# A hybrid decoder layer on one core: merge gates moved into a phase of their own, made by Strassen's seven block products

## The chip, the cores and the metric

The kernel runs on one core of a Trainium2 chip. The core has TensorE (PE) for matmuls, VectorE (DVE), ScalarE (ACT), GpSimd (POOL) and SyncE (SP), which here issues every DMA. The metric is the time of one execution in microseconds on the device, the median of three runs.

## What is computed

One step of a decoder layer for 1056 tokens: 1024 of a prompt and 8 x 4 of a decode batch, with shared weights. Cut to what matters here:

```python
xn = rmsnorm(x, norm_mix)
proj = xn @ w_in            # 1024 -> 512 (B) | 512 (C) | 512 (h) | 1536 (q,k,v) | 512 (z) | 8 | 512 (q_mem) | 3 x 1024 gates
y_a  = b_gate * causal_conv(c_gate * h_in)                    # branch A
o_dn = rmsnorm(gated_delta_chunked(q, k, v, g, beta, s0))     # branch B: a recurrence over chunks
y_dn = o_dn * jax.nn.silu(z)
y_m  = mem_attention(xq, mk, mv)                              # branch M
merged = (jax.nn.sigmoid(g_a) * (y_a @ w_branch[:512])
          + jax.nn.sigmoid(g_dn) * (y_dn @ w_branch[512:1024])
          + jax.nn.sigmoid(g_m) * (y_m @ w_branch[1024:]))
x = x + merged @ w_o
gate, up = jnp.split(rmsnorm(x, norm_ffn) @ w_up, 2, axis=-1)
y = rmsnorm(x + (jax.nn.silu(gate) * up) @ w_down, norm_final)
```

New convolution and recurrence states and the memory's keys and values are returned too.

## The kernel before

All large products are exact to float32 by three matmuls in fp32r: a weight and an activation are each split into a high and a low part (`split`: ScalarE casts the high part, VectorE subtracts), and high x high, high x low and low x high are added in one PSUM bank. `X` holds both parts of the normed input, transposed (8 tiles of 128 channels by 1056 tokens). `proj` (lines 266 to 277) makes 128 output columns over one of three token tiles `TT` (384, 384 and 288 tokens): 8 channel tiles by three matmuls, 24 in all, at lines 274 to 276.

The program has four stages. *The weave* (up to line 1119) lays four streams of work into each other by a clock of guessed costs (`weave`, `UNIT`, and the factors `SCS`, `DNS`, `ATS`); a scheduler then orders each engine's instructions by priority against a simulated timeline. The streams are: `bulk_all`, plain column products in the sequence of the string `ORDER` (X: the memory branch's queries, K: memory keys and values, L: a DeltaNet head's q, k, v, A: branch A, M and B: gates and branch products of the memory branch and branch A, G: gates of the DeltaNet branch, Z: its z columns); `dn_prep_all`, for each of 8 halves (4 heads by 2) a triangular inverse, whose 31 steps on VectorE (`dn_solve`, lines 489 to 491) run between two trips through DRAM, then `dn_levels` on TensorE; `dn_scan_all`, the recurrence; and `att_all`, attention and the decode tokens. In this stage matmuls of the three latter streams stand between the bulk's, on TensorE's in-order queue.

In the weave, `branch` (1009 to 1032) makes for each of 8 column tiles the gate (24 matmuls a token tile, then sigmoid, line 1024) and the branch product (12 a token tile), multiplies them and stores the result in DRAM (`dM`, `dAo`). `gate_d` (1034) keeps 8 gate tiles of the DeltaNet branch in SBUF (`sgD`), and `z_part` (984) makes y = o * silu(z).

*The merge* (1163 to 1183) makes the DeltaNet branch's products, multiplies them with `sgD`, adds `dM` and `dAo`, and splits the sum into `X`. Then *w_o with the second norm* (from 1296), *up* (from 1352) and *down* (from 1522). The up projection already takes seven block products for eight: `up_pieces` makes the sums of weight blocks, `combine` those of activations (T1 to T4), and `up_chunk` has the products, each 4 channel tiles by three matmuls on 256 or 272 tokens (lines 1425 to 1427). For it the late stages have four raw weight buffers and eight piece buffers (`ring_t`).

## Time and profile before

| | us |
|---|---|
| median of 3 runs (1891.04 to 1895.27) | 1892.73 |
| the profiled execution | 1891.13 |
| its span | 1889.4 |
| PE busy | 1851.5 |
| DVE busy | 1060.4 |
| ACT busy | 707.1 |
| POOL busy | 133.0 |

The span runs from the first to the last instruction of the profiled execution. A matmul's busy time is from its issue to the modelled end of its results, and overlaps the next; the distance between starts is what it costs in a stream. The weave lasts to 998 us, where the merge's first matmul stands; w_o begins at 1045 us, up at 1146 us and down at 1611 us.

### The profile page before, as it was taken

What the parts mean: (1) busy time and instruction counts of PE and PEld (TensorE: products, weight loads), DVE (VectorE), ACT (ScalarE), POOL (GpSimd) and SP (SyncE); (2) the same over time, 40 slices, a digit from 0 to 9 for tenths busy, and PEclk for the clock granted to TensorE, in tenths of its full rate; (3) what the DMA queues carried; (4) which work ended last, traced back from release to release, by engine and by line L of the source; (5) the groups of instructions that cost most, each with busy time, mean ns of one, the idle gap of its engine ahead of it and who ended that gap; (6) DMA issues with size and microseconds to landing.
All of it is one profiled execution on the core that took longest, in us unless ns stands there. A gap on an engine that the chain in (4) does not pass through costs nothing.

```text
span 1889.4 us, 31322 instructions
## 1 busy us (share of the span) xinstructions
PE 1851.5 (98%) x12193; PEld 1719.1 (91%) x12193; DVE 1060.4 (56%) x2543; ACT 707.1 (37%) x1520; POOL 133.0 (7%) x234
## 2 busy tenths in 40 slices
PE   6999999999999999999999999999999999999997
PEld 6799999889999999999999879999999999787776
DVE  6666568454744357721137567666766668536224
ACT  5533453234423343233232366433333335433121
POOL 3100011010100012100005000000000000001000
PEclk9999999999999999999999999999999999999999
DMA  5123122341322215431155445232323234846321
GB/s 175 34 71 82 48 62 78 114 138 52 110 74 80 89 42 136 125 94 55 52 171 170 162 149 186 73 94 72 94 72 94 74 93 149 271 142 211 107 85 65
DMA packets 224705, 200.43 MB, mean 106 GB/s; under 512 B 21332, under 2 KB 182025, under 8 KB 224556
## 3 DMA queue, kind: packets, MB, share of 16 engines
q1 hardware_dynamic: 224556, 198.43, 34.0%
q8 instruction: 95, 1.56, 0.4%
q14 instruction: 54, 0.44, 0.1%
HBM read 160.27 MB, written 38.12 MB: 105 GB/s over the span
## 4 chain that ended last, share of the span: by engine, by line
PE 93%; DVE 2%; DMA 2%; ACT 1%; issue 1%; SPq 0%; DVEq 0%; ACTq 0%
PE psb L274 14%; PE psb L275 13%; PE psb L276 13%; PE psb L1427 7%; PE psb L1425 7%; PE psb L1426 7%; PE psb L1281 6%; PE psb L1280 6%; PE psb L1282 6%; PE psb L1364 2%; DMA x<-in_x_prompt_dram 1%; PE psa L926 1%; PE psb L1284 1%; PE psb L1285 1%; PE psa L906 1%
## 5 line engine op out<-in xcount | busy, mean ns | idle before, releaser
L274 PE MATMUL psb<-x,whi 128*128 128x384 f32 (+1 forms) x1272 | 418.3, 329 | 1.6 <-ACT whi L103 1.2
L276 PE MATMUL psb<-x,wlo 128*128 128x384 f32 (+1 forms) x1272 | 415.1, 328 | 0.5 <-DVE wlo L96 0.5
L275 PE MATMUL psb<-x,whi 128*128 128x384 f32 (+1 forms) x1272 | 415.3, 327 | 0.0
L96 DVE TENSOR_TENSOR pc<-raw,pc 128x512 fp32r<-128x512 f32 (+1 forms) x237 | 198.0, 845 | 155.8 <-ACT pc L103 153.8
L103 ACT CAST pc<-raw 128x512 fp32r<-128x512 f32 (+1 forms) x237 | 174.0, 745 | 260.6 <-PE psb L1281 115.2
L274 PEld LDWEIGHTS psb<-x,whi 128*128 128x128 f32 x1272 | 239.6, 188 | 5.3 <-issue 1.9
L276 PEld LDWEIGHTS psb<-x,wlo 128*128 128x128 f32 x1272 | 239.9, 189 | 3.3 <-DVE wlo L96 1.2
L275 PEld LDWEIGHTS psb<-x,whi 128*128 128x128 f32 x1272 | 239.8, 189 | 3.1 <-issue 2.0
L96 DVE TENSOR_TENSOR wlo<-raw,whi 128x1024 fp32r<-128x1024 f32 x73 | 90.6, 1241 | 111.1 <-ACT whi L103 107.0
L1426 PE MATMUL psb<-bx,pc 128*128 128x272 f32 (+1 forms) x480 | 136.4, 285 | 0.0
L1427 PE MATMUL psb<-bx,pc 128*128 128x272 f32 (+1 forms) x480 | 136.3, 286 | 0.0
L1281 PE MATMUL psb<-pc,hx 128*128 128x512 f32 x344 | 136.1, 396 | 0.0
L1425 PE MATMUL psb<-bx,pc 128*128 128x272 f32 (+1 forms) x480 | 135.9, 286 | 0.0
L1282 PE MATMUL psb<-pc,hx 128*128 128x512 f32 x344 | 135.9, 395 | 0.0
L1280 PE MATMUL psb<-pc,hx 128*128 128x512 f32 x344 | 135.6, 394 | 0.0
L93 DVE TENSOR_TENSOR ev<-psb,ev 128x272 f32<-128x272 f32 (+1 forms) x208 | 89.5, 431 | 63.1 <-PE psb L1427 46.7
L103 ACT CAST whi<-raw 128x1024 fp32r<-128x1024 f32 x73 | 76.6, 1049 | 89.0 <-PE psb L275 70.6
L1425 PE MATMUL psb<-bx1T,pc 128*128 128x272 f32 x352 | 101.4, 288 | 1.6 <-DVE ev L93 1.6
L1427 PE MATMUL psb<-bx1T,pc 128*128 128x272 f32 x352 | 101.1, 288 | 0.0
L1426 PE MATMUL psb<-bx1T,pc 128*128 128x272 f32 x352 | 100.9, 287 | 0.0
L1426 PEld LDWEIGHTS psb<-bx,pc 128*128 128x128 f32 x480 | 91.0, 190 | 0.0
L1427 PEld LDWEIGHTS psb<-bx,pc 128*128 128x128 f32 x480 | 90.7, 189 | 0.0
(499 smaller groups left out, 3829.6 us busy)
## 6 DMA issues: line engine op xcount, KB each, us to landing
raw<-in_w_in_dram SPq DMA_DIRECT2D x56, 512.0 KB, 3.8
raw<-in_w_ffn_up_dram SPq DMA_DIRECT2D x56, 512.0 KB, 4.3
raw<-in_w_ffn_down_dram SPq DMA_DIRECT2D x44, 512.0 KB, 3.4
raw<-in_w_o_dram SPq DMA_DIRECT2D x16, 512.0 KB, 5.8
raw<-in_w_branch_dram SPq DMA_DIRECT2D x12, 512.0 KB, 3.5
dH<-ev SPq DMA_DIRECT2D x44, 136.0 KB, 1.7
hr<-dH SPq DMA_DIRECT2D x22, 272.0 KB, 3.5
...
```

What stands on the lines that cost most here:

```text
L93: eng.tensor_tensor(out, a, b, op=ALU.add)
L96: eng.tensor_tensor(out, a, b, op=ALU.subtract)
L103: A.copy(hi, src)
L274: T.matmul(o, w_h, xh[k][:, cs], start=k == 0, stop=False)
L275: T.matmul(o, w_h, xl[k][:, cs], start=False, stop=False)
L276: T.matmul(o, w_l, xh[k][:, cs], start=False, stop=k == nk - 1)
L1280: T.matmul(b, xh, wh, start=first, stop=False)
L1281: T.matmul(b, xh, wl, start=False, stop=False)
L1282: T.matmul(b, xl, wh, start=False, stop=last)
L1425: T.matmul(b, w[:, 0, k], x[:, 0, k], start=start and k == 0, stop=False, skip_group_check=not start)
L1426: T.matmul(b, w[:, 0, k], x[:, 1, k], start=False, stop=False, skip_group_check=not start)
L1427: T.matmul(b, w[:, 1, k], x[:, 0, k], start=False, stop=k == 3, skip_group_check=not start)
```

## The change

The gates of the M and B branches, of the DeltaNet branch, the z columns and all branch products leave the weave and the merge. `gate_fill` keeps ten plain gate columns in the weave (8 of branch A, 2 of the memory branch: `G8 G2`), stored in DRAM (`dG`). A new phase after the weave makes the rest, with six PSUM banks: the z columns of heads 0 and 1 plainly (`gate_plain`); the products of branch A with stored gates; the z columns of heads 2 and 3, the last six gate columns of the memory branch and the eight of the DeltaNet branch two columns at a time by seven block products (`gate_pair`), each followed by its branch products (`branch_pair`). The sums of activations for it (T1 to T4) are made in the weave by POOL (`tprep`), kept in DRAM (`dT`), and loaded and split in the new phase (`t_load`; T1 takes the place of a part of `X`). Attention results (`dYM`), y of the DeltaNet branch (`dYD`), o of the decode tokens and the merged columns (`dY2`) go through DRAM. The last pair is split into `X` directly; six columns are loaded back and split. The main pool has 9 slots in place of 13 with 3 more for the convolutions (`C`), two sigmoid tiles in place of 3; the solve's buffers are doubled. The late pools have 3 raw and 9 piece buffers and are open from the phase's start. `up_pieces` becomes `pair_pieces`, unchanged within.

```diff
-NSLOT = 13
+NSLOT = 9
+NC_ = 3
+DBUF = dict(Mt=3, Z=2, At=2, w1=2)
-SCS = 1.2
+SCS = 1.4
-ORDER = "X0 X1 K0 K1 A0 K2 X2 X3 K3 L1 A1 A2 A3 L2 M8 B1 L3 B7 G8 Z0 Z1 Z2 Z3"
-DNS = 0.8
+ORDER = "X0 K0 K1 K2 K3 X1 L1 A0 L2 X2 A1 X3 L3 A2 T0 T1 T2 T3 A3 G8 G2"
+DNS = 1.4
...
+    def gate_fill():
+        for f in range(2 * KT):
+            w = wcols(w_in[0], 0, KT, W_G + (f // KT) * 2048 + (f % KT) * P, P)
             for t in range(3):
                 t0, n = TT[t]
+                sg = sig_tile()[:, :n]
+                A.activation(sg, proj(*w, t), AF.Sigmoid)
+                nc.sync.dma_start(dG[f][:, t0:t0 + n], sg)
                 yield UNIT
...
+    GRP = ((slice(0, 256), slice(256, 512)), (slice(512, 784), slice(784, 1056)))
+    GN = (256, 272)
...
+    def tprep(kk):
+        x1, x2 = (C([P, NTOK], "xs") for _ in range(2))
+        for x, k in ((x1, kk), (x2, kk + 4)):
+            add(G, x, Xh[k].bitcast(F32), Xl[k].bitcast(F32))
+            yield 0.5
+        for g in range(2):
+            t1, t2 = GRP[g]
+            sub(G, x1[:, t1], x1[:, t2], x1[:, t1])
+            sub(G, x1[:, t2], x2[:, t2], x1[:, t2])
+            sub(G, x2[:, t2], x2[:, t2], x1[:, t1])
+            sub(G, x2[:, t1], x2[:, t1], x2[:, t2])
+            for p, t in (("T1", x1[:, t1]), ("T3", x1[:, t2]), ("T2", x2[:, t2]), ("T4", x2[:, t1])):
+                nc.sync.dma_start(dT[g][p][:, kk], t)
+            yield 0.5
...
+    def prod(b, w, x, start):
+        for k in range(4):
+            T.matmul(b, w[:, 0, k], x(0, k), start=start and k == 0, stop=False, skip_group_check=not start)
+            T.matmul(b, w[:, 0, k], x(1, k), start=False, stop=False, skip_group_check=not start)
+            T.matmul(b, w[:, 1, k], x(0, k), start=False, stop=k == 3, skip_group_check=not start)
...
+    def gv(n):
+        return gp.tile([P, 272], F32, tag="gv", bufs=9, name=nm("gv"))[:, :n]
...
+    def gate_pair(g, W, func):
+        n = GN[g]
+        ba, bb, bc, be = (bank("b")[:, :n] for _ in range(4))
+        out = {}
+        prod(ba, W["11"], xop(g, "11"), True)
+        p1_ = gv(n)
+        A.copy(p1_, ba)
+        prod(bb, W["S2"], xop(g, "T2"), True)
+        u2 = gv(n)
+        add(V, u2, bb, p1_)
+        prod(bc, W["S3"], xop(g, "T3"), True)
+        u3 = gv(n)
+        add(V, u3, bc, u2)
+        prod(be, W["S1"], xop(g, "T1"), True)
+        c = out["22"] = gv(n)
+        add(V, c, be, u3)
+        A.activation(c, c, func)
+        prod(ba, W["12"], xop(g, "21"), False)
+        c = out["11"] = gv(n)
+        A.activation(c, ba, func)
+        prod(bc, W["22"], xop(g, "T4"), False)
+        c = out["21"] = gv(n)
+        add(V, c, bc, u2)
+        A.activation(c, c, func)
+        prod(be, W["S4"], xop(g, "22"), False)
+        c = out["12"] = gv(n)
+        add(V, c, be, u2)
+        A.activation(c, c, func)
+        return out
+
+    def branch_pair(g, fs, wb, Y, sg, dst, pms, final=False):
+        n = GN[g]
+        hi, lo = wb
+        for key, j, th in BL:
+            cs = GRP[g][th]
+            b = bank("b")[:, :n]
+            c = slice(j * P, j * P + P)
+            for k in range(4):
+                T.matmul(b, hi[:, k, c], Y[k][:, 0, cs], start=k == 0, stop=False)
+                T.matmul(b, hi[:, k, c], Y[k][:, 1, cs], start=False, stop=False)
+                T.matmul(b, lo[:, k, c], Y[k][:, 0, cs], start=False, stop=k == 3)
+            s_ = sg[key]
+            mul(V, s_, b, s_)
+            for pm in pms:
+                m = gv(n)
+                with tc.high_priority(offset=AHEAD):
+                    nc.sync.dma_start(m, pm[fs[j]][:, cs])
+                add(V, s_, s_, m)
+            if final:
+                split(X[fs[j]][:, 0, cs], X[fs[j]][:, 1, cs], s_)
+            else:
+                nc.sync.dma_start(dst[fs[j]][:, cs], s_)
...
+    z_pair(0, True)
+    Y = []
+    for f in range(0, 8, 2):
+        for _ in br_pair(0, f, Y, dY, dA_, ready=f < nfill[0]):
+            pass
+        if f == 0:
+            for g in range(2):
+                for p in ("T2", "T3", "T4", "T1"):
+                    t_load(g, p)
+    z_pair(2)
+    Y = []
+    for f in range(0, 8, 2):
+        for _ in br_pair(2, f, Y, dYM, dM, ready=8 + f < nfill[0]):
+            pass
...
+    Y = []
+    for f in range(0, 8, 2):
+        for g, _ in br_pair(1, f, Y, dYD, dY2, (dM, dA_)):
+            if f == 6:
+                cs = slice(0, 512) if g == 0 else slice(512, 1056)
                 with tc.high_priority(offset=AHEAD):
+                    for k in range(6):
+                        raw = raw_t()[:, :cs.stop - cs.start]
+                        nc.sync.dma_start(raw, dY2[k][:, cs])
+                        split(X[k][:, 0, cs], X[k][:, 1, cs], raw)
```

TensorE's queue before, in the last gate column of `gate_d`: `psb` is the PSUM bank, `x0` and `x1` tiles of `X`, `whi` and `wlo` the weight's two parts.

```order
L274 MATMUL psb_1369_9845<-x0_74,whi_1364_9787 128x288
L275 MATMUL psb_1369_9845<-x0_74,whi_1364_9787 128x288
L276 MATMUL psb_1369_9845<-x0_74,wlo_1365_9788 128x288
L274 MATMUL psb_1369_9845<-x1_75,whi_1364_9787 128x288
L275 MATMUL psb_1369_9845<-x1_75,whi_1364_9787 128x288
L276 MATMUL psb_1369_9845<-x1_75,wlo_1365_9788 128x288
```

TensorE's queue in the changed kernel, in the z columns of heads 2 and 3, at the end of the first and the start of the second block product (`pc_1310` and `pc_1311` are pieces of the weight, `tx0T2` is a T piece):

```order
L1155 MATMUL psb_1317_9001<-x3_77,pc_1310_8978 128x256
L1156 MATMUL psb_1317_9001<-x3_77,pc_1310_8978 128x256
L1157 MATMUL psb_1317_9001<-x3_77,pc_1310_8978 128x256
L1155 MATMUL psb_1318_9002<-tx0T2_8031,pc_1311_8982 128x256
L1156 MATMUL psb_1318_9002<-tx0T2_8031,pc_1311_8982 128x256
L1157 MATMUL psb_1318_9002<-tx0T2_8031,pc_1311_8982 128x256
```

A product takes four tiles of `X` or of a T piece on 256 tokens, where the column before took eight on 384 or 288; two columns have seven products for each of two groups of tokens.

TensorE's queue in the changed kernel, at the second pair of branch A's products: `y` are the branch's input tiles, `pc_1255` is the branch weight's high part, `pc_1256` its low part.

```order
L1219 MATMUL psb_1237_8472<-y_1220_8344,pc_1225_8355 128x272
L1217 MATMUL psb_1257_8559<-y_1211_8317,pc_1255_8554 128x256
L1218 MATMUL psb_1257_8559<-y_1211_8317,pc_1255_8554 128x256
L1217 MATMUL psb_1258_8574<-y_1211_8317,pc_1255_8554 128x256
L1218 MATMUL psb_1258_8574<-y_1211_8317,pc_1255_8554 128x256
L1217 MATMUL psb_1259_8589<-y_1211_8317,pc_1255_8554 128x256
L1218 MATMUL psb_1259_8589<-y_1211_8317,pc_1255_8554 128x256
L1217 MATMUL psb_1260_8604<-y_1211_8317,pc_1255_8554 128x256
L1218 MATMUL psb_1260_8604<-y_1211_8317,pc_1255_8554 128x256
L1217 MATMUL psb_1265_8627<-y_1211_8317,pc_1255_8554 128x272
L1218 MATMUL psb_1265_8627<-y_1211_8317,pc_1255_8554 128x272
L1217 MATMUL psb_1266_8642<-y_1211_8317,pc_1255_8554 128x272
L1218 MATMUL psb_1266_8642<-y_1211_8317,pc_1255_8554 128x272
L1219 MATMUL psb_1257_8559<-y_1211_8317,pc_1256_8555 128x256
```

The products of six blocks with the high part stand ahead of the first with the low part (line 1219), where in the pair before each block runs through in turn.

SP's queue in the changed kernel, ahead of that pair's weight (`raw_1254`):

```order
L1291 DMA dYD0_8037<-gv_1198_8237 128x272
L1253 DMA raw_1249_8539<-dT1T1_858 128x544
L1291 DMA dYD1_8038<-gv_1200_8264 128x272
L1291 DMA dYD0_8037<-gv_1202_8291 128x272
L1301 DMA gv_1231_8421<-dG0_815 128x272
L1301 DMA gv_1232_8423<-dG1_816 128x272
L1118 DMA raw_1254_8553<-in_w_branch_dram 128x4x256
L1301 DMA gv_1233_8425<-dG0_815 128x272
L1301 DMA gv_1250_8545<-dG3_818 128x256
L1118 DMA raw_1273_8695<-in_w_branch_dram 128x4x256
L1118 DMA raw_1292_8837<-in_w_branch_dram 128x4x256
L1230 DMA dAo1_840<-gv_1207_8309 128x256
```

The last T piece (line 1253), stores of y (1291) and loads of gates (1301) stand ahead of the weight (1118); stores of the first pair's results (1230) come behind it, with the weights of the third and fourth pairs.

## Rows read from the trace of the kernel before

**Rows 1.** The page, part 1: busy us, share of the span, instructions.

```profile
PE 1851.5 (98%) x12193; PEld 1719.1 (91%) x12193; DVE 1060.4 (56%) x2543; ACT 707.1 (37%) x1520; POOL 133.0 (7%) x234
```

**Rows 2.** Windows: length, then busy us of each engine (instructions), clock, DMA.

```profile
core 0: us, PE busy (x) PEld busy (x) DVE busy (x) ACT busy (x) POOL busy (x), PEclk, DMA share, GB/s
0.00:100.00 100.00, 81.06 (x474) 72.04 (x475) 64.22 (x148) 53.02 (x109) 21.47 (x49) 0.97 0.33 99
100.00:600.00 500.00, 500.00 (x3469) 466.42 (x3467) 298.60 (x916) 192.17 (x474) 40.19 (x73) 1.00 0.29 84
600.00:1000.00 400.00, 394.36 (x2597) 383.98 (x2598) 164.81 (x435) 134.17 (x297) 38.78 (x64) 1.00 0.32 95
1200.00:1300.00 100.00, 100.00 (x817) 100.00 (x817) 67.61 (x132) 30.83 (x64) 0.00 (x0) 1.00 0.26 78
1600.00:1700.00 100.00, 96.59 (x448) 79.27 (x447) 50.35 (x66) 40.64 (x60) 1.85 (x8) 1.00 0.64 210
```

**Rows 3.** Timeline of PE: start us, duration, line, tiles (first, last).

```profile
929.91 0.34 PE L274 MATMUL psb<-x,whi 128*128 128x384 f32 x1
...
934.94 0.34 PE L276 MATMUL psb<-x,wlo 128*128 128x384 f32 x1
...
936.15 0.29 PE L274 MATMUL psb<-x,whi 128*128 128x288 f32 x1
...
939.20 0.30 PE L276 MATMUL psb<-x,wlo 128*128 128x288 f32 x1
...
1300.46 0.29 PE L1426 MATMUL psb<-bx,pc 128*128 128x272 f32 x1
...
1302.95 0.29 PE L1425 MATMUL psb<-bx1T,pc 128*128 128x272 f32 x1
```

**Rows 4.** Chain of waits, 1140 to 1200 us: start us, length, what.

```profile
1166.12 22.67 PE psb L1364 x189
```

**Rows 5.** Waits of PE, 600 to 1000 us: total, times, longest.

```profile
PE psb L274 <- ACT sg L995: 1.3, 1, 1.3
PE psb L274 <- ACT sg L1024: 0.9, 1, 0.9
```

**Rows 6.** Windows of 20 us, columns as in rows 2.

```profile
1020.00:1040.00 20.00, 20.00 (x128) 20.00 (x127) 19.65 (x28) 4.71 (x10) 15.85 (x17) 1.00 0.61 216
1600.00:1620.00 20.00, 16.59 (x105) 14.89 (x104) 16.04 (x28) 11.36 (x18) 0.00 (x0) 1.00 0.93 315
```

**Rows 7.** Solve steps (line 491) and o stores: ns, first and last start.

```profile
L491 DVE TENSOR_REDUCE w<-w x31: 154/223/287, 118.1 to 145.3; 128x4 f32<-128x8 f32 x1, 128x4 f32<-128x12 f32 x1, 128x4 f32<-128x16 f32 x1, 128x4 f32<-128x20 f32 x1
L491 DVE TENSOR_REDUCE w<-w x31: 163/225/283, 354.7 to 385.8; 128x4 f32<-128x8 f32 x1, 128x4 f32<-128x12 f32 x1, 128x4 f32<-128x16 f32 x1, 128x4 f32<-128x20 f32 x1
L491 DVE TENSOR_REDUCE w<-w x31: 160/218/289, 504.3 to 529.9; 128x4 f32<-128x8 f32 x1, 128x4 f32<-128x12 f32 x1, 128x4 f32<-128x16 f32 x1, 128x4 f32<-128x20 f32 x1
L491 DVE TENSOR_REDUCE w<-w x31: 165/222/289, 559.5 to 582.7; 128x4 f32<-128x8 f32 x1, 128x4 f32<-128x12 f32 x1, 128x4 f32<-128x16 f32 x1, 128x4 f32<-128x20 f32 x1
L598 SPq DMA_DIRECT2D dO<-ot x8: 319/338/420, 242.2 to 909.9; - x8
```

**Rows 8.** Groups by line and form: busy us, mean ns, idle before.

```profile
L96 DVE TENSOR_TENSOR pc<-raw,pc 128x512 fp32r<-128x512 f32 x168 | 114.2, 690 | 38.3 <-ACT pc L103 36.5
L103 ACT CAST pc<-raw 128x512 fp32r<-128x512 f32 x168 | 102.5, 621 | 141.7 <-PE psb L1427 104.6 <-DVE raw L96 17.2 <-issue 7.0
L96 DVE TENSOR_TENSOR pc<-raw,pc 128x1024 fp32r<-128x1024 f32 x69 | 83.8, 1223 | 117.5 <-ACT pc L103 117.2 <-PE psb L1282 0.2
L93 DVE TENSOR_TENSOR ev<-psb,ev 128x272 f32<-128x272 f32 x110 | 48.4, 440 | 10.8 <-PE psb L1427 3.3 <-issue 2.6
```

**Rows 9.** DMA issues: count, KB each, median us to landing.

```profile
raw<-in_w_in_dram SPq DMA_DIRECT2D x56, 512.0 KB, 3.8
raw<-in_w_ffn_up_dram SPq DMA_DIRECT2D x56, 512.0 KB, 4.3
dAo<-sg SPq DMA_DIRECT2D x16, 192.0 KB, 3.9
```

More of the change, by code (lines that the diff above doesn't have):

```diff
@@ L457, in dn_prep @@
         yield 3
-        e, r, tm, sc = [dn.tile([P, 8], F32, tag=f"dn_sm{i}", bufs=3, name=nm("dsm")) for i in range(4)]
+        e, r, tm, sc = [dn.tile([P, 8], F32, tag=f"dn_sm{i}", bufs=4, name=nm("dsm")) for i in range(4)]
         V.tensor_scalar(e, ss, EPS, None, op0=ALU.add)
@@ L856, in dn_decode @@
         A.activation(osm.rearrange("p h t -> p (h t)"), b[:, :P], AF.Copy, scale=hc[:, 60:61])
+        for h in range(H):
+            nc.sync.dma_start(dO[h][:, NP:NTOK], osm[:, h])
         yield 3
@@ new lines, in prod @@
+    def prod(b, w, x, start):
[3 more added lines that the diff above has]
+            T.matmul(b, w[:, 1, k], x(0, k), start=False, stop=k == 3, skip_group_check=not start)
+    mctx.close()
+    yctx, yp = sub_pool("yp")
+    gctx, gp = sub_pool("gp")
+    tctx, tp = sub_pool("tp")
+    TX = [{p: tp.tile([P, 2, 4, GN[g]], F32R, name=f"tx{g}{p}") for p in ("T2", "T3", "T4")} for g in range(2)]
@@ new lines, in load_hl, with y_load @@
+    def load_hl(dst, src):
+        with tc.high_priority(offset=AHEAD):
+            for cs in (slice(0, 512), slice(512, 1056)):
+                raw = raw_t()[:, :cs.stop - cs.start]
+                nc.sync.dma_start(raw, src[:, cs])
+                split(dst[:, 0, cs], dst[:, 1, cs], raw)
+    def y_load(src):
+        ys = []
+        for f in range(4):
+            y = yp.tile([P, 2, NTOK], F32R, tag="y", bufs=4, name=nm("y"))
+            load_hl(y, src[f])
+            ys.append(y)
+        return ys
@@ new lines, in t_load @@
+    def t_load(g, p):
+        with tc.high_priority(offset=AHEAD):
+            n = GN[g]
+            step = 4 if g == 0 else 2
+            for k in range(0, 4, step):
+                raw = raw_t()[:, :step * n].rearrange("p (k c) -> p k c", k=step)
+                nc.sync.dma_start(raw, dT[g][p][:, k:k + step])
+                if p == "T1":
+                    for i in range(step):
+                        x = X[k + i][:, :, GRP[g][1]]
+                        split(x[:, 0], x[:, 1], raw[:, i])
+                else:
+                    split(TX[g][p][:, 0, k:k + step], TX[g][p][:, 1, k:k + step], raw)
@@ new lines, with gate_plain @@
+    Wg = w_in[0]
+    ga = lambda i, f: W_G + 1024 * i + f * P
+    def gate_plain(g, ws, func):
+        n = GN[g]
+        out = {}
+        for key, j, th in BL:
+            hi, lo = ws[j]
+            b = bank("b")[:, :n]
+            cs = GRP[g][th]
+            for k in range(KT):
+                T.matmul(b, hi[:, k], X[k][:, 0, cs], start=k == 0, stop=False)
+                T.matmul(b, hi[:, k], X[k][:, 1, cs], start=False, stop=False)
+                T.matmul(b, lo[:, k], X[k][:, 0, cs], start=False, stop=k == KT - 1)
+            c = out[key] = gv(n)
+            A.activation(c, b, func)
+        return out
@@ new lines, in z_pair @@
+    def z_pair(f, plain=False):
+        if plain:
+            W = [split_cols(Wg, W_Z + f * P + j * P, KT, P) for j in range(2)]
+        else:
+            W = pair_pieces(Wg, W_Z + f * P, W_Z + f * P + P)
+        for g in range(2):
+            sg = (gate_plain if plain else gate_pair)(g, W, AF.Silu)
+            for key, j, th in BL:
+                cs = GRP[g][th]
+                o = gv(GN[g])
+                with tc.high_priority(offset=AHEAD):
+                    nc.sync.dma_start(o, dO[f + j][:, cs])
+                mul(V, sg[key], sg[key], o)
+                nc.sync.dma_start(dYD[f + j][:, cs], sg[key])
@@ new lines, in br_pair @@
+    def br_pair(i, f, ys, src, dst, pms=(), ready=False):
+        W = None if ready else pair_pieces(Wg, ga(i, f), ga(i, f + 1))
+        for g in range(2):
+            if ready:
+                sg = {}
+                for key, j, th in BL:
+                    sg[key] = gv(GN[g])
+                    with tc.high_priority(offset=AHEAD):
+                        nc.sync.dma_start(sg[key], dG[4 * i + f + j][:, GRP[g][th]])
+            else:
+                sg = gate_pair(g, W, AF.Sigmoid)
+            if g == 0:
+                if not ys:
+                    ys.extend(y_load(src))
+                wb = split_cols(w_branch[0, 512 * i:512 * i + 512], f * P, 4, 256)
+            yield g, branch_pair(g, (f, f + 1), wb, ys, sg, dst, pms, final=i == 1 and f == 6)
@@ L1144 @@
+    z_pair(0, True)
[4 more added lines that the diff above has]
+        if f == 0:
+            for g in range(2):
+                for p in ("T2", "T3", "T4", "T1"):
[5 more added lines that the diff above has]
+            pass
     w_o_pre = []
```

236 lines of the change are left out of this document (84 added, 152 removed).

## The prediction

> **What bounds the kernel now.** I read the page first. TensorE's matmuls are busy for 98% of the span, VectorE for 56% [rows 1], and the windows show where the missing 2% lies [rows 2]: nothing is lost from 100 to 600 us, 5.6 us are lost between 600 and 1000 us, nothing in the SwiGLU's up projection (1200 to 1300 us), 3.4 us where the down projection starts (1600 to 1700 us), some 19 us in the first 100 us. The granted clock is 1.00 (2.4 GHz) in all of them but the first. So the time is the sum of the matmuls' spacings, and a change is worth the matmul time that it removes, less the waits that it makes. What a matmul costs is not its own duration, which overlaps its neighbours', but the distance from one start to the next [rows 3]: 173.4 ns for 384 columns (934.94 less 929.91 us over 29 steps), 132.6 ns for 288 (3.05 us over 23), 124.5 ns for 272 (2.49 us over 20). For 256 columns the chain of waits has 189 of them in 22.67 us, 120 ns each [rows 4]. The cost follows the columns, with some 10 ns on top that do not.
>
> **What the change does to TensorE's own work.** A gate or z column of 128 outputs takes 24 matmuls over each of three token tiles (384, 384, 288): 24 x (173.4 + 173.4 + 132.6) = 11.51 us. By the scheme, two columns and a group of tokens take 7 block products of 12 matmuls; over both groups (blocks of 256 and of 272 tokens) that is 84 x (120 + 124.5) = 20.54 us for two columns, 10.27 us for one. The driver takes 16 of the 28 gate and z columns that way (2 of z, 6 of the memory branch, 8 of the DeltaNet branch): the first ten gate columns are made in the weave as before, and the first z pair is plain. Gain: 16 x 1.24 = 19.8 us, not an eighth, because narrower matmuls pay the fixed part more often.
>
> Against it: the plain z pair runs on blocks of 256 and 272, 24 x 2 x 244.5 ns = 11.74 us a column, 0.23 us more, twice: 0.5 us. All 24 branch columns (12 matmuls over each block) go the same way, from 12 x 479.4 ns = 5.75 to 24 x 244.5 ns = 5.87 us: 24 x 0.115 = 2.8 us. The net is **16.6 us** less on TensorE. All else it does is the same.
>
> Here a rule speaks against the change. The Trainium skill ("TensorE: Matmul & The Clock Gate", section "Back-to-back issue gap") puts the sustained spacing at 81 ns for 128 columns and 131 ns for 512. On a straight line between the two, an estimate from that page, 256 columns would cost 98 ns and 384 would cost 114 ns, and what the narrower blocks lose would be some 27 us more than what the scheme saves. The rows here contradict it: 120 ns and 173 ns [rows 3, 4].
>
> **Waits that go.** From 600 to 1000 us TensorE waited 1.3 us for a silu tile of the z columns and 0.9 us for a sigmoid tile of a branch (lines 995 and 1024) [rows 5]. Both lines are gone: 2.2 us. The other waits in those rows are on weights or the scan and may stay.
>
> **Waits that come.** The new phase moves much more through DRAM: the attention result, gates, T pieces, z results and merged columns. All of it is issued from SP's one queue, and stores and loads stand in each other's way there. *First place: the second pair of branch 0.* Ahead of its weight in SP's order stand the eight pieces of y, all twelve loads of T pieces, o and gate loads and 11 stores, 11.2 MB with the weight. Sizes and counts come from the issues' shapes. They can start about 6 us before the weave's last matmul, and until the pair is due TensorE has 6.1 + 2 x 11.74 + 2 x 5.87 = 41.3 us of work. At the 315 GB/s that the queue moved when the down projection started [rows 6] they take 35.5 us; at the 216 GB/s of 1020 to 1040 us, 51.8 us. The wait lies between 0 and 10.5 us. The order expects a late one: it puts the high-part matmuls of six blocks ahead of the first low-part one. I take 4 us, by the nearest row: at 315 GB/s TensorE still waited 3.4 us [rows 6]. What hides the T pieces themselves is branch 0, 4 x 11.74 = 47 us.
>
> *Second: the rest of the phase.* VectorE for one pair of the last branch: 11 sums and low parts on 512 columns at 0.69 us, one low part of 1024 at 1.22, 10 sums out of PSUM, 8 products and 16 sums at about 0.43, together 23.4 us beside 32.3 us of matmuls, 72%. The up projection runs at 68% with TensorE never idle [rows 2, 8]: VectorE does not become the bound, nor ScalarE, whose casts take 0.62 us each [rows 8]. At a change of branch, eight y pieces and three weights go through three raw buffers; a weight lands in 3.8 us and a store of this kind in 3.9 [rows 9]. Between 0 and 6 us; I take 2 us, about two of the single waits in [rows 5].
>
> *Third: the weave.* It loses 14 gate columns, 4 of z and 16 branch columns, 14 x 11.51 + 4 x 11.51 + 16 x 5.75 = 299 us of matmuls, which were the cover of the DeltaNet chain. That chain ran from 118 to 910 us with room to spare: from the fourth solve's last step at 385.8 to the fifth's first at 504.3 it only waited for its place in the order [rows 7]. Where two halves followed closely, their solves started 55.2 us apart (504.3, 559.5), without a wait of TensorE [rows 2, 7]. In the new order successive halves stand 55 to 60 us of matmul time apart, the last two closer, with double buffers for the solve. A solve's steps took 23.2 to 31.1 us [rows 7]; a slow one would come some 2 us late past the spare time. Seven halves: 0 to 14 us. I take 1.5, since the tight pairs of before show none. The last scan ends 14 us of gate matmuls before the weave does. POOL gets 40 more operations (the T pieces), behind which its DeltaNet steps queue; TensorE waits for none of them directly, and the upper end of 14 us holds them.
>
> At nothing I cost three raw buffers in place of four in the later stages: one up block needs three, and its 7.6 us of piece making plus 4.3 us of loading [rows 8, 9] fit into its 20.5 us; without that cover it costs a load's 4 us where the down projection begins.
>
> **Sum.** The profiled execution took 1891.1 us (span 1889.4). 1891.1 - 16.6 - 2.2 + 4 + 2 + 1.5 = 1879.8 us. It stands 1.6 us below the median of the three runs, so I forecast **1881.4 us**.
>
> **Rivals.** (a) *The first stretch of the new phase is bound by its transfers.* From the first y piece to the end of branch 0, 21.5 MB move beside 76.6 us of matmuls: 281 GB/s, more than the 210 GB/s of the busiest 100 us [rows 2]. For it: SP's queue in order, loads that wait for the landing of stores, nine small buffers. Against it: 315 GB/s in one stretch [rows 6]. If it moves at 216 GB/s it takes 99.5 us, 23 us more, in place of the 4 us: 1881.4 - 4 + 22.9 = 1900 us, **slower**. It decides from about 234 GB/s down: there the phase's first 21.5 MB take 15.3 us too long, which is all that the other terms gain.
> (b) *The gain is eaten by many small waits* (each branch change, each half): 12 us more than I took, about half of what the three upper ends leave; 1893 us, no change.
> (c) *The DeltaNet chain becomes the bound.* If each of seven halves stretches by the 4 us between the slowest and the first solve (31.1 and 27.2 us) [rows 7] with no spare time, 28 us in place of 1.5: 1908 us. Against it: the tight pairs.
> (d) *A matmul costs by its number, not by its columns.* The order has 525 more rows for TensorE; at 120 ns each and nothing saved on columns that is 63 us more, 1950 us. [rows 3] speak against it clearly. By that page's line (Trainium skill, same section) it would be about 1924 us, and the trace does not bear it out.
> (e) *All waits stay at nothing, and the weave loses its 5.6 us of idle time as well:* 1891.1 - 16.6 - 5.6 + 1.6 = 1870.5 us; the lower end.
>
> **Chances.** My forecast with its own range of 1871 to 1889 us, (e) within it: 0.61. (b): 0.16. (a): 0.16. (c): 0.06. (d): 0.01. A measurement can tell some 0.2%, 3.8 us, from no change: faster means below 1888.9, slower above 1896.5. Faster 0.61, same 0.16, slower 0.23. The range runs from 1871 to 1900 us: it takes in (b) and about half of (a).
>
> **What would show it.** In the new profile: 84 x 2 matmuls a pair at lines 1155 to 1157 spaced 120 and 125 ns; one wait of some 4 us at lines 1217 to 1219 on a weight's low or high part at the second pair of branch 0, with the DMA share near 0.9 there; the weave's end some 299 us earlier, with TensorE full up to it; no wait of TensorE longer than 2 us elsewhere. Wrong would be: waits on y pieces or gate loads throughout branch 0 (then a), waits at lines 526 to 580 spread over the weave (then c), or a spacing of 256-column matmuls far from 120 ns with two operands read from X (then the first term).

## The result, and the profile after

The changed kernel took 1921.61 us (median of 4 runs, 1919.27 to 1924.97), the kernel before 1892.38 us beside it: ratio 1.0152, 95% interval 1.0138 to 1.0166. It is 29 us slower, where 11 us less were forecast, and outside the range of 1871 to 1900 us. The profiled execution's span is 1920.7 us against 1889.4.

The page, part 1, and the windows of the changed kernel (length, then busy us of each engine and instructions, clock, DMA share, GB/s):

```profile
PE 1849.1 (96%) x12721; PEld 1709.8 (89%) x12721; DVE 1159.9 (60%) x2784; ACT 734.8 (38%) x1614; POOL 142.7 (7%) x246
```

```profile
0.00:100.00 100.00, 78.92 (x447) 68.41 (x447) 58.07 (x144) 50.12 (x98) 25.49 (x57) 0.97 0.32 99
100.00:480.00 380.00, 374.39 (x2552) 344.43 (x2553) 268.84 (x876) 171.93 (x460) 33.06 (x69) 0.99 0.26 74
480.00:560.00 80.00, 70.83 (x556) 61.23 (x556) 69.53 (x152) 22.72 (x65) 54.68 (x57) 0.98 0.50 155
560.00:720.00 160.00, 157.07 (x1087) 150.99 (x1086) 63.32 (x225) 57.11 (x154) 19.41 (x33) 1.00 0.41 121
720.00:1073.00 353.00, 334.50 (x2711) 332.38 (x2710) 207.07 (x407) 114.09 (x218) 1.82 (x6) 0.99 0.57 172
1200.00:1300.00 100.00, 99.95 (x820) 99.73 (x819) 71.22 (x148) 46.71 (x105) 0.00 (x0) 1.00 0.26 79
1600.00:1700.00 100.00, 96.69 (x553) 84.47 (x552) 60.71 (x98) 44.39 (x73) 0.47 (x2) 0.98 0.63 199
```

Against [rows 1, 2]: TensorE's busy time hardly fell, and it is idle in places where it was not: 9.2 us of 80 from 480 to 560 us, 18.5 us of 353 in the new phase. In the first of these VectorE is busy 87% and POOL 68%. In the kernel before, the same 80 us had VectorE at 57% and POOL at 4%:

```profile
480.00:560.00 80.00, 80.00 (x531) 77.94 (x530) 45.68 (x156) 29.30 (x54) 3.42 (x4) 1.00 0.35 101
```

The block products cost what was expected. Timeline of PE in the changed kernel, first and last of 60 matmuls of 256 columns (start us, duration, line, tiles); 6.97 us over 59 steps are 118 ns, beside the 120 of [rows 4]:

```profile
874.74 0.28 PE L1155 MATMUL psb<-x,pc 128*128 128x256 f32 x1
...
881.71 0.28 PE L1157 MATMUL psb<-x,pc 128*128 128x256 f32 x1
```

TensorE's longest waits in the whole span (us in total, times, longest):

```profile
PE psb L1217 <- ACT pc L108: 12.7, 2, 9.3
PE psp L232 <- DMA At<-in_conv_a_w_dram: 8.5, 1, 8.5
PE pss L216 <- DVE x L194: 6.9, 4, 3.3
PE psa L983 <- DMA t<-in_cache_mem_v_dram: 4.4, 4, 2.9
PE psb L1217 <- DVE gv L95: 3.5, 3, 1.6
PE pss L575 <- DVE vt L104: 3.3, 3, 2.1
PE psb L663 <- DVE wlo L101: 3.1, 1, 3.1
```

The second and third stand in the head of both kernels. Of the first, 9.3 us are the place that the prediction named first, and 3.4 us stand at 949 us, on the first branch weight of the third branch.

To see where the time went I split it. For each matmul I took the distance to the next start. Its *work* is the usual distance for its form, by both kernels (120, 125, 132, 175 and 233 ns for 256, 272, 288, 384 and 512 columns; the lower quartile for short forms). The rest is *loss* (the expectations call it excess): waits, half clock (a granted clock of 0.5, 1.2 GHz), short steps without cover. Work and losses add up to the span less some 18 us, the time before the first matmul and after the last. The last scan step is the last matmul of line 575 (569 in the kernel before). In us, for one profiled execution each (for e9, e14 and e15 the fastest of their runs, for e17 the slowest), the median beside it:

| kernel | median | work | loss: first 100 us | rest of weave | new phase | later | last scan step at |
|---|---|---|---|---|---|---|---|
| before | 1892.4 | 1777.8 | 22.1 | 66.6 (with merge) | - | 4.7 | 895 |
| changed | 1921.6 | 1760.1 | 25.8 | 87.5 | 20.1 | 8.5 | 695 |
| e9 | 1915.4 | 1760.1 | 21.6 | 76.8 | 26.2 | 7.3 | 675 |
| e12 | 1916.2 | 1760.1 | 22.8 | 86.7 | 16.5 | 9.9 | 691 |
| e14 | 1903.3 | 1762.6 | 22.0 | 70.0 | 15.6 | 8.4 | 670 |
| e15 | 1890.3 | 1760.1 | 23.2 | 70.9 | 4.1 | 8.0 | 672 |
| e17 | 1910.8 | 1757.5 | 24.8 | 77.2 | 27.8 | 6.6 | 680 |

So the work fell by 17.7 us, and the loss rose by 48.5 us: 3.7 in the first 100 us (kernels with the same head lose 21.6 to 25.8 there, so this is mostly scatter), 20.9 in the weave, 20.1 in the new phase, 3.8 later.

### The profile page after: what moved, and what is told of

Read it like the earlier page. It is cut to its first block, busy times and chain, and to the rows that moved or that the text cites. A ratio compares the mean times of both kernels' runs of the same rounds, so it can differ in the third digit from the quotient of the medians.

```text
span 1920.7 us, 33436 instructions
## 1 busy us (share of the span) xinstructions
PE 1849.1 (96%) x12721; PEld 1709.8 (89%) x12721; DVE 1159.9 (60%) x2784; ACT 734.8 (38%) x1614; POOL 142.7 (7%) x246
## 5 line engine op out<-in xcount | busy, mean ns | idle before, releaser
L101 DVE TENSOR_TENSOR pc<-raw,pc 128x512 fp32r<-128x512 f32 (+1 forms) x307 | 254.1, 833 | 195.0 <-ACT pc L108 96.6
L108 ACT CAST pc<-raw 128x512 fp32r<-128x512 f32 (+1 forms) x307 | 224.4, 738 | 360.6 <-PE psb L1157 128.7
L280 PE MATMUL psb<-x,whi 128*128 128x384 f32 (+1 forms) x840 | 278.2, 332 | 2.0 <-DVE u L95 2.0
L281 PE MATMUL psb<-x,whi 128*128 128x384 f32 (+1 forms) x840 | 276.9, 330 | 0.0
L282 PE MATMUL psb<-x,wlo 128*128 128x384 f32 (+1 forms) x840 | 275.5, 329 | 0.0
L280 PEld LDWEIGHTS psb<-x,whi 128*128 128x128 f32 x840 | 158.0, 188 | 5.6 <-DVE u L95 2.3
L281 PEld LDWEIGHTS psb<-x,whi 128*128 128x128 f32 x840 | 158.0, 188 | 3.4 <-issue 2.2
L282 PEld LDWEIGHTS psb<-x,wlo 128*128 128x128 f32 x840 | 158.1, 188 | 3.2 <-issue 2.2
L1217 PE MATMUL psb<-y,pc 128*128 128x256 f32 (+1 forms) x384 | 110.6, 288 | 16.2 <-ACT pc L108 12.7
L1218 PE MATMUL psb<-y,pc 128*128 128x256 f32 (+1 forms) x384 | 110.1, 287 | 0.0
L1219 PE MATMUL psb<-y,pc 128*128 128x272 f32 (+1 forms) x384 | 108.1, 285 | 0.0
L1155 PEld LDWEIGHTS psb<-bx,pc 128*128 128x128 f32 x480 | 90.8, 189 | 1.6 <-ACT ev L1557 1.6
```

The costliest lines, as they stand in the source:

```text
L101: eng.tensor_tensor(out, a, b, op=ALU.subtract)
L108: A.copy(hi, src)
L280: T.matmul(o, w_h, xh[k][:, cs], start=k == 0, stop=False)
L281: T.matmul(o, w_h, xl[k][:, cs], start=False, stop=False)
L282: T.matmul(o, w_l, xh[k][:, cs], start=False, stop=k == nk - 1)
L1155: T.matmul(b, w[:, 0, k], x(0, k), start=start and k == 0, stop=False, skip_group_check=not start)
```

## The experiments

Times are medians; the ratio is to the kernel before, measured beside it. e1 to e8 and e12 start from the changed kernel (e7 from e1); from e9 on, but for e12, edits are added up. Differences of 3 to 5 us between two edits mostly lie within their intervals; there the waits in the trace carry the reading.

**Is it cover, SP's queue, or the order of the weave's parts?** Three edits of the weave:

```diff
e2 -ORDER = "... T0 T1 T2 T3 A3 G8 G2"   +ORDER = "... T0 T1 T2 T3 A3 G8 G8"
e3 -nc.sync.dma_start(dT[g][p][:, kk], t)  +nc.gpsimd.dma_start(dT[g][p][:, kk], t)
e4 +ORDER = "X0 X1 K0 K1 A0 K2 X2 X3 K3 L1 A1 A2 A3 L2 T0 T1 T2 T3 L3 G8 G2"
```

> One edit: all 16 gate columns of branches 0 and 2 stay in the weave as plain columns (10 before the edit), so 6 columns fewer go by block products. Known price: 6 columns x (11.51 - 10.27) us = +7.4 us of matmul time. Theory 1 (the weave lost its cover: DeltaNet's and attention's short steps have too few long matmuls beside them): about 69 us more of long matmuls in the weave take its losses beyond spacing from 113 us (0 to 722 us) down by 10 to 18 us, time 1911 to 1919 us. Rival (the weave's losses come from the new work on POOL and SP, or from the new order of its parts): losses stay within 4 us, time 1925 to 1930 us.

1929.35 us, ratio 1.0183 (1.0165 to 1.0202), the rival's time. The weave's loss stayed (90.6 us after its first 100 us, against 87.5). The last scan step stood at 695 us as before: the six columns came behind the chain and covered nothing. Columns at the end of the list are no cover.

> One edit: the 32 stores of T pieces in the weave are issued by POOL, which makes them, not by SP. Theory 1 (in SP's queue they wait for POOL, 12.7 us in 13 waits at 480-556 us, and hold up the loads of cached values behind them, for which TensorE waits 4.4 us and then runs 3.4 us at half clock): 5 to 7 us less in the weave, 1914 to 1917 us. Rival (loads are late for want of buffers, or the loss is lost cover): within 2 us of 1921.6.

1957.49 us, ratio 1.0332 (1.0316 to 1.0348): both expectations fail: it is 36 us slower than the changed kernel, all of it in the weave (loss 122.5 us). Each of the 32 issues held POOL for 539 to 736 ns, 18 us in all. That pointed at POOL's time, not SP's.

> One edit: the weave's list of parts in the order it had before the change (X0 X1 K0 K1 A0 K2 X2 X3 K3 L1 A1 A2 A3 L2, then T0 to T3, L3, G8, G2). Theory 1 (loss of cover, whatever the order): within 3 us of 1921.6. Rival (the new order of the head: first 100 us lose 25.8 us instead of 22.1, lines 661 and 663 wait 5.2 us in 100-130 us where before they waited 0.9): 8 us back, 1912 to 1915 us.

1997.72 us, ratio 1.0564 (1.0533 to 1.0595). DeltaNet's loads come late, its last scan step stands at 783 us, behind the weave's last column, and TensorE waits 14.1 us at once at line 478: the chain needs the new order. But the rival was right about its place. From 100 to 150 us, the kernel before, the changed kernel and e4:

```profile
100.00:150.00 50.00, 50.00 (x339) 48.19 (x338) 36.48 (x131) 15.42 (x38) 2.27 (x4) 1.00 0.27 69
100.00:150.00 50.00, 44.39 (x309) 42.53 (x310) 33.35 (x114) 20.08 (x52) 2.08 (x2) 0.93 0.37 98
100.00:150.00 50.00, 50.00 (x345) 49.52 (x345) 34.10 (x121) 14.40 (x35) 2.11 (x2) 1.00 0.26 70
```

In the changed kernel TensorE waited there 5.1 us for the weights of the memory keys and values (lines 661 and 663), and from 120 to 140 us its clock was 0.83. By the split, these 50 us lose some 11 us, against 2 before and under 1 in e4. So the head's new order costs some 8 us, which e4 won back and lost many times over later. No run kept the chain early without that price.

**POOL against VectorE.** By time, 22.6 us of the weave's loss lie from 484 to 554 us, where the kernel before lost 1.8 (both by the split above). That is where POOL makes the T pieces. The groups of VectorE by form in the changed kernel, first before that stretch (300 to 480 us), then in it (count, busy us, mean ns, idle before):

```profile
L104 DVE SCALAR_TENSOR_TENSOR vt<-pss,ned,vt 128x128 f32<-128x128 f32 x9 | 3.1, 349 | 2.0 <-PE pss L570 1.5 <-ACT wk L923 0.3 <-issue 0.2
L104 DVE SCALAR_TENSOR_TENSOR yA<-u,hc,yA 128x1072 f32<-128x1072 f32 x2 | 2.6, 1312 | 4.0 <-DMA raw<-in_w_in_dram 4.0
L95 DVE TENSOR_TENSOR wk<-qsm,bm 128x128 f32<-128x128 f32 x8 | 2.2, 288 | 3.8 <-PE psa L958 3.8
```

```profile
L95 DVE TENSOR_TENSOR wk<-t,bm 128x128 f32<-128x128 f32 x16 | 10.5, 708 | 0.6 <-PE psa L983 0.5
L104 DVE SCALAR_TENSOR_TENSOR yA<-u,hc,yA 128x1072 f32<-128x1072 f32 x2 | 5.1, 2573 | 0.0
L104 DVE SCALAR_TENSOR_TENSOR vt<-pss,ned,vt 128x128 f32<-128x128 f32 x4 | 1.4, 342 | 2.9 <-ACT psp L456 2.9
```

Operations with two operands in SBUF (wk, yA) take 2.5 and 2.0 times as long; one that reads PSUM (vt) takes the same. Five operations with a single SBUF operand, of 4 or 8 columns (lines 115, 116, 465 and 609), were slow too: 0.62 to 2.38 us, where their like took 0.16 to 0.17 us from 300 to 480 us. Against the durations of the same forms elsewhere, VectorE's 126 operations of that stretch took some 24 us more. Two edits test it, the place and the engine:

```diff
e5 +ORDER = "X0 K0 K1 K2 K3 X1 L1 A0 L2 X2 A1 X3 L3 A2 A3 G8 G2 T0 T1 T2 T3"
e6 -add(G, x, Xh[k]...)  -sub(G, x1[:, t1], ...)   +add(V, x, Xh[k]...)  +sub(V, x1[:, t1], ...)
```

> One edit: the preparation of the T pieces (POOL) stands last in the weave's list, behind the gate columns, where VectorE is busy 31% (600-700 us) instead of 78% (500-600 us). Theory 2 (while POOL works on T pieces, VectorE's operations on SBUF operands take longer, 23.8 us more in 484-554 us by their own durations elsewhere; VectorE is then busy 19.45 of 20 us and TensorE waits for it): the same SBUF operations of VectorE are swollen again, but where it has slack, so the weave's excess of 87.5 us falls by 14 to 20 us: 1902 to 1908 us. Rival (lost cover, or SP's queue with the 32 stores): within 4 us of 1921.6.

1920.75 us, ratio 1.0146 (1.0131 to 1.0161): the time is the rival's, the mechanism is not. The order put the T work at 543 to 621 us, not at 600 to 700, beside other dense steps of VectorE, and the swelling went with it. So did the loss: by the split some 9 us less from 500 to 550 us, some 12 us more from 550 to 600. Its groups from 484 to 543 us (no T work), then from 543 to 621 us:

```profile
L95 DVE TENSOR_TENSOR wk<-t,bm 128x128 f32<-128x128 f32 x16 | 3.7, 285 | 3.4 <-PE psa L983 3.1 <-ACT t L973 0.3
L95 DVE TENSOR_TENSOR w<-w,Ab 128x116 f32<-128x116 f32 x1 | 0.4, 356 | 0.0
```

```profile
L104 DVE SCALAR_TENSOR_TENSOR yA<-u,hc,yA 128x1072 f32<-128x1072 f32 x2 | 4.9, 2426 | 0.0
L95 DVE TENSOR_TENSOR w<-w,Ab 128x116 f32<-128x116 f32 x1 | 2.2, 2197 | 0.0
```

> One edit: the 40 additions and subtractions for the T pieces go to VectorE, at the same place of the list. Theory 2 (VectorE and POOL hold each other up): durations of VectorE's other SBUF operations are back at their normal size (128x128 product wk<-t,bm 288 ns instead of 708), but VectorE takes on about 23 us of its own work (8 x 1.3 us + 32 x 0.38 us), so the time stays within 5 us of 1921.6 (1917 to 1926). Rival (POOL's own queue, its DeltaNet operations late behind T work): 1904 to 1910 us.

1916.41 us, ratio 1.0123 (1.0108 to 1.0138). The product wk<-t,bm is back at 326 ns and the weave's loss fell to 76.1 us, as theory 2 has it; VectorE was busy 57.48 us of the 70 against 61.29, although it does the T work itself. The stores stayed (DMA share 0.52 and 0.54), so they are not what slowed VectorE. The windows of the changed kernel and of e6, then the product in e6:

```profile
484.00:554.00 70.00, 60.83 (x485) 51.89 (x484) 61.29 (x129) 20.10 (x60) 53.50 (x55) 0.98 0.52 165
484.00:554.00 70.00, 69.28 (x558) 63.11 (x558) 57.48 (x180) 21.87 (x66) 8.26 (x15) 1.00 0.54 167
L95 DVE TENSOR_TENSOR wk<-t,bm 128x128 f32<-128x128 f32 x16 | 4.4, 326 | 0.0
```

The time fell by only 5 us, since the weave then ended at 705 us, 7 us behind the last scan step, and TensorE waited 9.7 us for the first weight of the new phase.

**The wait in branch 0.** Edits e1, e7 and e8:

```diff
e1 -if f == 0: for g in range(2): ... t_load(g, p)   +if f in (2, 4): ... t_load(f // 2 - 1, p)
e7 e1, and in t_load  -with tc.high_priority(offset=AHEAD):  +with tc.high_priority(offset=0):
e8 -nc.sync.dma_start(dYD/dst ..., sg[key]/s_)  +nc.gpsimd.dma_start(dYD/dst ..., sg[key]/s_)
```

> One edit: the 12 loads of the T pieces of x go out after pairs f=2 (g=0) and f=4 (g=1) of branch 0, not all after f=0. Theory 1 (the weight of pair f=2 lands late because the T pieces stand ahead of it in SP's queue and in the ring of three raw buffers): the wait of 9.5 us at 759 us and its 10.2 us at half clock go, 9 to 12 us in all, and no wait above 2 us takes their place: 1910 to 1913 us against 1921.6. Rival (the whole stretch is bound by the rate of transfers, 304 GB/s at 760-780 us, so bytes only move): the wait shows up at another pair, time 1918 to 1922 us.

1919.24 us, ratio 1.0134 (1.0118 to 1.015). The weight of pair f=2 now stood ahead of the T loads, and the one long wait was gone; but the T loads were issued as early as before (733 to 761 us), and smaller waits on gate products came instead (8.2 us in six). Undecided, since the edit moved both the weight's turn and too little of the traffic.

> One edit: the stores of z outputs and of branch partial sums in the new phase are issued by POOL, idle there, instead of SP. Theory 3 (SP's queue, where stores wait for VectorE, 51 us in 29 waits in the new phase, holds up the loads behind them): the excess of the new phase falls by 6 to 12 us, 1910 to 1916 us. Rival (rate of transfers): within 3 us of 1921.6; if POOL's issues slow VectorE as its arithmetic does: 2 to 6 us slower.

1920.17 us, ratio 1.0145 (1.0128 to 1.0162), loss of the new phase 20.3 us: stores in SP's queue are not the cause.

> e1 with the loads of T pieces no longer issued ahead of their place in the program: in SP's order 6 of the 8 loads of g=1 now stand behind branch 0's gate loads and stores, where in e1 all 12 stayed ahead of the weight of pair f=2. Theory 1 (too many transfers in 733-780 us): the excess of the new phase falls from 20.1 us (18.7 in e1) to 8 to 12 us, 1910 to 1914 us. Rival (gate loads are late because they wait in SP's queue for gv buffers whose stores have not landed): excess stays at 16 us or more, 1917 to 1921 us.

1928.75 us, ratio 1.0189 (1.0173 to 1.0204), neither: one wait of 19.5 us, on the weight of the fourth pair. (The expectation has e1 wrong: there the weight of pair f=2 was asked for at 731.7 us, ahead of the first T load at 733.0.) The issues in SP's queue (start us, length, line, transfer), the T loads of line 1253 and that weight, both through the three `raw` buffers:

```profile
788.01 0.42 SPq L1253 DMA_DIRECT2D raw<-dT1T  x1
790.58 0.42 SPq L1253 DMA_DIRECT2D raw<-dT1T  x1
791.21 0.38 SPq L1118 DMA_DIRECT2D raw<-in_w_branch_dram  x1
```

The later the T loads, the later the weight: it gets one of the three raw buffers only in its turn, behind the T pieces, although here its load has the higher priority. In the changed kernel it is the same, the last T load at 759.00 us, the weight at 762.77 us, with TensorE idle since 759.5 us (`gv` are nine small tiles):

```profile
759.00 0.32 SPq L1253 DMA_DIRECT2D raw<-dT1T  x1
759.36 0.94 SPq L1291 DMA_DIRECT2D dYD<-gv  x2
761.88 0.80 SPq L1301 DMA_DIRECT2D gv<-dG  x2
762.77 0.38 SPq L1118 DMA_DIRECT2D raw<-in_w_branch_dram  x1
```

e12 gives the weights their buffers first, nothing else:

```diff
+        if f == 0:
+            for f1 in (2, 4, 6):
+                WB[f1] = split_cols(w_branch[0, :512], f1 * P, 4, 256)
```

> The changed kernel with one edit: the weights of pairs f=2, 4 and 6 of branch 0 take their raw buffers ahead of the T pieces, all else as it was (12 T loads, POOL's work in the weave). Theory 4 (the three raw buffers are handed out in program order, so the weight of the second pair waits until 12 T pieces have been landed and split): the wait of 9.5 us at 759 us goes, the T pieces land later but in time for the z pair at 836 us; the excess of the new phase falls from 20.1 to 9 to 12 us: 1909 to 1914 us. Rival (rate of transfers, 304 GB/s there): the excess stays above 16 us, 1918 to 1922 us.

1916.23 us, ratio 1.0125 (1.0108 to 1.0143). The wait on the weight is gone, but half of it came back on gates: TensorE's waits and the window of e12 there:

```profile
PE psb L1217 <- DVE gv L95: 5.5, 3, 2.9
```

```profile
760.00:780.00 20.00, 16.33 (x121) 15.69 (x121) 12.92 (x27) 5.63 (x11) 0.00 (x0) 0.94 0.96 292
```

The loss of the phase fell by 3.6 us, not by 8 to 11. At a DMA share of 0.96 and 292 GB/s the rate may well be the second limit behind the ring, but no run parts it from the gate loads' own wait for `gv` buffers.

**Without the traffic.** In e9 VectorE makes the T pieces in the new phase out of x in SBUF (line 1247's t_load replaced); e10 and e11 add to it, e13 adds the weights of e12:

```diff
e9  +add(V, raw, X[k][:, 0, cs].bitcast(F32), X[k][:, 1, cs].bitcast(F32))   (both halves, in raw buffers)
    +sub(V, a, b, a); sub(V, b, d, b); sub(V, d, d, a); sub(V, c, c, d); then split into TX and X
    -T0 T1 T2 T3 in ORDER, -dT, -t_load
e10 e9, G8 G2 -> G8 G4      e11 e10, wb = split_cols(...) ahead of y_load      e13 e11 and the edit of e12
```

> The T pieces are made in the new phase, by VectorE from the halves of x that lie in SBUF, after pairs f=0 (g=0) and f=2 (g=1) of branch 0: no POOL work and no 32 stores in the weave, no 12 loads (4.3 MB) in the new phase. Theory 2 for the weave (POOL against VectorE): the weave's excess falls from 87.5 us to 72 to 76 us, as in e6 (76.1). Theory 1 for the new phase (T loads stand ahead of the weight of pair f=2): the wait of 9.5 us and its half clock go; its rival (that wait comes from the y pieces, gate loads and z weights alone): 6 us or more stay. The weave then ends near 705 us, with DeltaNet's chain, and the first weight of the new phase is waited for about 10 us, as in e6. Sum by both theories: 1921.6 - 13 - 10 + 10 = 1908 us (1904 to 1912); by the rival 1914 to 1920 us.

1915.35 us, ratio 1.0123 (1.0099 to 1.0146), the rival's time. The weave's loss fell by 10.7 us to 76.8, near what was expected, and with it the chain: TensorE is busy all of 484 to 524 us, where it was idle for 5.6. The two rows are of the changed kernel and of e9:

```profile
484.00:524.00 40.00, 34.38 (x239) 29.61 (x237) 38.69 (x85) 9.73 (x29) 30.34 (x28) 1.00 0.40 124
```

```profile
484.00:524.00 40.00, 40.00 (x330) 35.19 (x328) 24.97 (x99) 15.12 (x47) 3.28 (x5) 1.00 0.40 117
```

The new phase did not gain: a wait of 13.3 us on the weight of the third pair of branch 0, now behind T pieces that use the raw buffers as scratch. No wait on the first weight came (weave's end 33 us behind the last scan step).

> e9 with 12 gate columns in the weave in place of 10. Price: 2 columns x (11.51 - 10.27) = +2.5 us. Theory (the first weight of the new phase is late only because its buffers come free when DeltaNet's chain ends, and columns behind that end hide the load): the 10 us of e9 before the first product of the phase go: e9 - 7 us, 1898 to 1904 us. Rival (that wait has nothing to do with the chain's end): e9 + 2 us.

1914.87 us, ratio 1.0112 (1.0096 to 1.0129): with no such wait in e9 there was nothing to win, and the price of 2.5 us is not to be told from the scatter.

> e10 with the first branch weight of each branch asked for ahead of the eight y pieces, not behind them. Theory (at 949 us the weight is the last of nine loads through three raw buffers): the wait of 3.6 us there falls to 0 to 1.5 us, and one like it at the first branch weight of branch 0: 2 to 4 us less than e10. Rival (the y pieces then land last in its place): within 1 us of e10.

1910.46 us, ratio 1.0084 (1.0065 to 1.0103): 4 us less; the waits at the change of branch (3.7 us at 940 us) and at the second pair of branch 0 (2.1 us) are gone, and one of 12.6 us is left, on a weight of branch 0.

> e11 with the weights of branch 0 ahead of the T pieces as in e12. Theory 4: the wait of 12.7 us at 778 us (the weight of pair f=4 behind 12 pairs of raw buffers that the T pieces use, VectorE 10.0 of 10 us busy at 770-780) goes: 8 to 13 us less than e11, 1898 to 1903 us. Rival (VectorE's work on the T pieces bounds the stretch wherever the weights stand): 3 us or less, 1907 to 1911 us.

1907.29 us, ratio 1.0082 (1.0062 to 1.0103): the wait on the branch weight went, and 5.7 us of it came up at 801 us, at the second z pair, whose pieces stand behind the T pieces in the same ring. The time is the rival's, and by the ratios (1.0084 and 1.0082) no gain over e11 is to be told; for theory 4 speaks only that the wait went to the next in the ring.

**Cover among the steps, and the ring once more.**

```diff
e14 e13, "... X3 L3 A2 A3 G8 G4" -> "... X3 L3 G2 A2 G2 A3 G8"
e15 e14, G2, G2, G6; W2 = pair_pieces(...) of the second z pair after pair f=4, ahead of the last two t_make of g=1
e16 e15 with G3, G3, G4          e17 e15 with G2, G2, G4
```

> e13 with 4 of the 12 gate columns spread between the parts of the weave that feed DeltaNet and attention (G2 ahead of A2, G2 ahead of A3, G8 last). Theory (what is left of the weave's loss, 75 us in e11 against 66 in the kernel before with 323 us more of matmuls, is lost cover: columns after the chain's end, 675 us, cover nothing, as e2 showed): 3 to 8 us less than e13, 1892 to 1899 us, with the chain's end later. Rival (the chain only ends later, and the first weights of the new phase with it): e13 or up to 5 us slower.

1903.29 us, ratio 1.006 (1.0043 to 1.0078). The weave's loss fell from 75.0 to 70.0 us; the last scan step even came 4 us earlier. Five kernels with one and the same weave (the changed kernel, e1, e7, e8, e12) differ by some 3 us in this loss, so 5 us is more than scatter, if not by much: columns among the steps do cover.

> e14 with the weight pieces of the second z pair ahead of the last two T pieces of g=1 in the ring of raw buffers, and 10 gate columns in the weave (G2, G2, G6) in place of 12. Theory 4 (ring order, third time): the wait of 6.1 us at 795 us falls below 1.5 us; 2 columns fewer as plain ones give 2.5 us: 6 to 9 us less than e14, 1894 to 1898 us. Rival (VectorE, near full at 765-790 us, bounds the stretch): 3 us less, 1899 to 1901 us.

1890.28 us (10 runs), ratio 0.9993 (0.9983 to 1.0003). The loss of the new phase is 4.1 us. TensorE's longest waits in it, e15 from 680 to 1038 us:

```profile
PE psb L1155 <- DVE gv L98: 1.3, 2, 0.8
PE psb L1155 <- DVE gv L95: 1.0, 2, 0.5
PE psb L1217 <- DVE gv L95: 0.6, 2, 0.3
```

It is 13 us less than e14, more than the wait and the two columns explain (8.6 us): the waits of 2.8 us at 835 and 3.0 us at 941 us went too. With all block products of the change it is 31 us faster than the changed kernel, and not to be told from the kernel before. Against that, its work is 17.7 us less, but its losses are still 12.8 us more, in the profiled executions.

> e15 with the 10 gate columns spread as G3, G3, G4. Theory of cover (long matmuls among DeltaNet's steps cost less than behind them): the weave's excess falls by another 1 to 3 us, 1891 to 1896 us. Rival (the chain's end sets when the first weights of the new phase can load, and fewer columns stand behind it): a wait of some us at the first products of the new phase, within 2 us of e15 or slower.

1891.32 us, ratio 0.999 (0.9981 to 0.9999): no difference to e15. The weave's loss (73.4 us) did not fall further.

> e15 with 8 gate columns in the weave (G2, G2, G4), so 18 columns by block products. Price by columns: 2 x (11.51 - 10.27) us = 2.5 us less than e15 (1890.3), 1887 to 1889 us, if no wait takes it back. Rival (DeltaNet's chain ends at 672 us in e15 and the columns behind it hide the first weights of the new phase; now the weave ends with the chain): a wait of 3 to 10 us at the first product of the new phase, 1890 to 1898 us.

1910.75 us, ratio 1.0092 (1.0075 to 1.0109), the rival and more. TensorE's waits, e17 from 640 to 760 us, and the window:

```profile
PE psb L1275 <- ACT pc L108: 8.6, 1, 8.6
PE pss L601 <- POOL ot L95: 4.6, 1, 4.6
```

```profile
680.00:700.00 20.00, 6.81 (x42) 6.17 (x41) 5.84 (x20) 5.08 (x9) 1.04 (x1) 0.67 0.44 126
```

The weave's last column now ends with the chain: nothing covers the last step of o, nor the load of the first z weights. That load goes out at 690.8 us, right behind the last store of o, for whose data SP's queue waited 5.5 us; whether the queue or a buffer held it was not separated. Two columns fewer in the weave turned a gain of 2.5 us into a loss of some 20.

## Why the prediction was wrong

**The first term was right.** Work fell by 17.7 us against the 16.6 us of the sum. Rival (d) is out; its sum was wrong besides, since by its own terms (1881.4 + 16.6 + 63) it gives 1961 us and not 1950. The estimate from the Trainium skill ("TensorE: Matmul & The Clock Gate", section "Back-to-back issue gap") was 1924 us, close to the measured time by coincidence: 118 ns for 256 columns agree with the rows, not with that line, and the work fell.

**The third term failed, and with it the sum.** The weave was given 1.5 us, bounds 0 to 14, and 2.2 us of waits were to go; it lost 20.9 us more after its first 100 us. The step that failed is the sentence on POOL: "40 more operations (the T pieces), behind which its DeltaNet steps queue". POOL's queue was costed, its effect on VectorE was not: those operations slowed VectorE's own ones on SBUF, by some 24 us in 70. Giving them to VectorE itself (e6) took 11.4 us of the 20.9 away, removing the T work (e9) 10.7.

The other 10 stay without any T work. Some 7 of them lie from 100 to 150 us (e9 loses 8.9 us there, the kernel before 2.2): the new order of the weave's head, which the prediction put at nothing without a reason. From 484 to 554 us e9 still loses 12 us more than the kernel before (14 against 1.8), and some 9 us less in the rest of its shorter weave. Spreading four columns among the steps (e14) won 5 us back, so that much is lost cover, which the term took at 1.5 us. What the rest is was not separated: the smaller pools (9 slots for 13, two sigmoid tiles for three) and the new factors of the weave's clock were never changed by themselves.

The Trainium skill has a rule that the prediction did not use ("SBUF — State Buffer", section "Who interferes with whom"): a VectorE instruction with two SBUF inputs contends with a GpSimd instruction that reads SBUF. The trace agrees: 288 to 708 ns with two SBUF inputs, 349 to 342 ns with PSUM among them. The five slow operations with one SBUF operand are not covered by that sentence.

**The first place was right in place, short in cause and size.** It was to be a wait of 4 us, bounds 0 to 10.5, on the weight of the second pair of branch 0; it was 9.3 us there, then matmuls of 256 columns 0.21 us apart for some 4 us at half clock (clock 0.74 from 760 to 780 us), 11 us in all. The price came from the rate of transfers. The runs show the turn in the ring of three raw buffers, in which a piece waits for a landing and a split: with the weights first (e12) this wait was gone. Yet the phase lost only 3.6 us less, so something else, perhaps the rate (292 to 304 GB/s), stood close behind. The half clock had no term.

**The second place** was given 2 us, bounds 0 to 6; it lost some 9 us, 3.4 of it on the third branch's first weight behind eight y pieces (949 us). That mechanism was named, its price too low.

**"At nothing"** stood the three raw buffers in the later stages: these lost 3.8 us more, half of it at the start of down, where 4 us were named for a lost cover. No run separated it.

Rival (a) named the right stretch, but it lost 11 us and not 23, and not by rate alone. Rival (b), many small waits in all places, does not describe it: most of the added loss sits in a few stretches, at 100 to 150, 484 to 554 and 759 to 773 us. Rival (c) comes near in size, 28 us for the weave, but not in mechanism: the weave of the changed kernel ended 28 us behind the last scan step, and only e17, two columns further on, ends with the chain.
